# First tile loaded whole with its own weights, second tile in pieces of 16 and 9 tokens, the other tiles' weights sent behind the first store

## The chip, the cores and the metric

The kernel runs on one core of one Trainium2 chip. The metric is the device time of one execution in microseconds (us). A tensor lies in the chip's main memory (HBM) and is worked on in the core's own memory (SBUF), which has 128 partitions. VectorE (DVE in the profile) and ScalarE (ACT) multiply; 16 DMA engines carry data between the two memories. A transfer is issued by the sequencer of an engine: here SyncE (SP) issues the stores and the weights, on the queue that the profile calls q1, and ScalarE issues the loads of `x`, on q10.

## The reference

Each token's row of 512 numbers is copied for each of its two experts and multiplied by that expert's weight. The expert indices are not used.

```python
batch, seq, hidden, n_experts = 16, 1024, 512, 8
k = 2
x_expanded = x[:, :, np.newaxis, :].repeat(k, axis=2)
weights = expert_weights[..., np.newaxis]
return (x_expanded * weights).astype(np.float32)
```

All is float32. There are 16,384 tokens, so 33.55 MB of `x` and 0.13 MB of weights come in, and 67.11 MB of output go out.

## The kernel before

With 128 partitions, each partition gets 128 tokens. They are cut into five tiles of 25 tokens for each partition (`groups`) and a rest of 3 (`LAST`, held in `z_tile`). Token counts below are always those of one partition. A tile of `x` is 128 rows of 25 × 2,048 bytes, and every transfer has one row for each partition, eight to each of the 16 DMA engines.

The buffers:

- `x_tile`: two buffers in turn, so tile i+2 can be loaded only when tile i has been multiplied.
- `o_ring`: one output buffer, as large as one whole tile's output (25 × 4,096 bytes a partition). Each part of a tile writes to its own range of it, so a part can be written only when the store of the range's last content has landed.
- `w_tile`: the weights of all tiles.

`load(i)` (L68) issues the loads of tile i on ACT's queue. For tile 0 it issues two, of 9 and 16 tokens (`FIRST`, L35), and behind the first of them it has SP issue all three weight transfers (L82-83): `weights(0)` (L95) for tile 0, 50 numbers a partition; `weights(1)` (L97) for tiles 1 to 4, four stretches of 50 numbers a partition; `weights(2)` (L104) for the rest, 6 numbers a partition. Then `load(0)` issues the load of `z_tile` (L85). `load(1)` issues tile 1 in one piece.

The main loop (L156) takes the tiles in order. `emit` (L148) cuts tiles 0 and 1 into 13 and 12 tokens and the later ones into 9, 8 and 8. For each part, `fill` (L142) has VectorE do the first v tokens, in steps of up to four tokens (one `tensor_tensor` each, L127), and ScalarE the rest, with one multiplication for each token and expert (L117). `SHARES` (L36) holds v: 9 of 13 and 8 of 12 in tiles 0 and 1; in later tiles VectorE does all. Then SP issues the part's store (L152). Below, the stores are called 0a and 0b (tile 0), 1a and 1b (tile 1), 2a, 2b, 2c and so on, and z for the last. After a tile's parts, `load(i + 2)` is issued from ACT's queue, which therefore stands behind that tile's multiplications on ScalarE.

Each queue is served in the order of issue: on SP the three weight transfers, then the stores in order; on ACT the loads of tile 0, z, tile 1, and then tiles 2, 3 and 4 as their buffers come free.

Of the kernel before, what the change touches and what calls it, by code (L numbers as in the profile page):

```python
# [1 line left out]

# [4 lines left out]


@with_exitstack
def kernel(  # L10
    ctx: ExitStack,
    tc: tile.TileContext,
    x: bass.AP,
    expert_indices: bass.AP,
    expert_weights: bass.AP,
    out: bass.AP,
):
    nc = tc.nc

    batch, seq, hidden = x.shape  # L20
    k = expert_weights.shape[-1]
    P = nc.NUM_PARTITIONS
    ntok = batch * seq
    assert ntok % P == 0
    A_TOTAL = ntok // P

    f32 = mybir.dt.float32
    row = k * hidden
    CH = 4


    groups = [25, 25, 25, 25, 25]
    TX = max(groups)
    LAST = 3
    FIRST = [9, 16]  # L35
    SHARES = [[9, 8], [9, 8], [9, 8, 8]]  # L36
    assert sum(groups) + LAST == A_TOTAL

    xf = x.rearrange("b s h -> (b s) h")
    of = out.rearrange("b s k h -> (b s) (k h)")  # L40
    wf = expert_weights.rearrange("b s k -> (b s) k")

    w_pool = ctx.enter_context(tc.tile_pool(name="w_pool", bufs=1))
    x_pool = ctx.enter_context(tc.tile_pool(name="x_pool", bufs=2))
    o_pool = ctx.enter_context(tc.tile_pool(name="o_pool", bufs=1))

    w_tile = w_pool.tile([P, A_TOTAL * k], f32)
    o_ring = o_pool.tile([P, TX * row], f32)

    def rows(of_all, done, T):  # L50
        return of_all[done * P : (done + T) * P, :].rearrange(
            "(p a) n -> p (a n)", a=T
        )


    if LAST:
        z_pool = ctx.enter_context(tc.tile_pool(name="z_pool", bufs=1))
        z_tile = z_pool.tile([P, LAST * hidden], f32)

    tiles = []  # L60
    done = 0
    for n in groups:
        tiles.append((done, n))
        done += n

    loaded = []

    def load(i):  # L68
        if i >= len(tiles):
            return  # L70
        done, n = tiles[i]
        x_tile = x_pool.tile([P, TX * hidden], f32)
        src = rows(xf, done, n)
        steps = FIRST if i == 0 else [n]
        for e, step in enumerate(steps):
            at = sum(steps[:e])
            nc.scalar.dma_start(
                out=x_tile[:, at * hidden : (at + step) * hidden],
                in_=src[:, at * hidden : (at + step) * hidden],
            )  # L80
            if i == 0 and e == 0:
                for g in range(3):  # L82
                    weights(g)
        if i == 0 and LAST:
            nc.scalar.dma_start(out=z_tile, in_=rows(xf, A_TOTAL - LAST, LAST))  # L85
        loaded.append(x_tile)


    T0 = groups[0]
    G = len([n for n in groups[1:] if n == T0])  # L90
    head = (1 + G) * T0

    def weights(e):
        if e == 0:
            nc.sync.dma_start(out=w_tile[:, : T0 * k], in_=rows(wf, 0, T0))  # L95
        elif e == 1:
            nc.sync.dma_start(  # L97
                out=w_tile[:, T0 * k : head * k].rearrange("p (g n) -> p g n", g=G),
                in_=wf[T0 * P : head * P, :].rearrange(
                    "(g p a) n -> p g (a n)", g=G, p=P  # L100
                ),
            )
        else:
            nc.sync.dma_start(  # L104
                out=w_tile[:, head * k :], in_=rows(wf, head, A_TOTAL - head)
            )

    def product(engine, o_tile, t, x_in, c, m):

        o = t * row  # L110
        if engine is not None:
            for e in range(m * k):
                out_e = o_tile[:, o + e * hidden : o + (e + 1) * hidden]
                in_e = x_in[:, e // k * hidden : (e // k + 1) * hidden]
                w_e = w_tile[:, c + e : c + e + 1]
                if engine is nc.scalar or engine is nc.any and (c + e) % 3 == 2:
                    nc.scalar.mul(out=out_e, in_=in_e, mul=w_e)  # L117
                else:
                    nc.vector.tensor_scalar(
                        out=out_e,  # L120
                        in0=in_e,
                        scalar1=w_e,
                        scalar2=None,
                        op0=mybir.AluOpType.mult,
                    )
            return
        nc.vector.tensor_tensor(  # L127
            out=o_tile[:, o : o + m * row].rearrange(
                "p (t k h) -> p t k h", t=m, k=k
            ),  # L130
            in0=x_in[:, : m * hidden]
            .rearrange("p (t h) -> p t h", t=m)
            .unsqueeze(2)
            .to_broadcast([P, m, k, hidden]),
            in1=w_tile[:, c : c + m * k]
            .rearrange("p (t k) -> p t k", t=m)
            .unsqueeze(3)
            .to_broadcast([P, m, k, hidden]),
            op=mybir.AluOpType.mult,
        )  # L140

    def fill(o_tile, x_in, c, m, v):  # L142
        for t in range(0, v, CH):
            u = min(t + CH, v)
            product(None, o_tile, t, x_in[:, t * hidden : u * hidden], c + t * k, u - t)
        product(nc.scalar, o_tile, v, x_in[:, v * hidden :], c + v * k, m - v)

    def emit(src, dst, c, cuts, shares):  # L148
        for at, to, v in zip(cuts, cuts[1:], shares):
            o_tile = o_ring[:, at * row : to * row]  # L150
            fill(o_tile, src[:, at * hidden : to * hidden], c + at * k, to - at, v)
            nc.sync.dma_start(out=dst[:, at * row : to * row], in_=o_tile)  # L152

    for i in range(2):
        load(i)
    for i, (done, n) in enumerate(tiles):  # L156
        cuts = [0, 13, n] if i < 2 else [0, 9, 17, n]
        emit(loaded[i], rows(of, done, n), done * k, cuts, SHARES[min(i, 2)])
        load(i + 2)
    emit(  # L160
        z_tile,
        rows(of, A_TOTAL - LAST, LAST),
        (A_TOTAL - LAST) * k,
        [0, LAST],
        [LAST],
    )

# [1 line left out]
_INS = ['x', 'expert_indices', 'expert_weights']  # L169
_OUTS = [((16, 1024, 2, 512), 'float32')]  # L170


# [23 lines left out]
```

## Time and profile before

| What | Value |
|---|---|
| Time, median of 3 runs | 240.13 us (239.79 to 240.28) |
| Time of the profiled execution | 240.12 us |
| Span of the profiled execution | 238.3 us |
| VectorE busy | 122.6 us (51% of the span), 32 instructions |
| ScalarE busy | 21.2 us (9%), 33 instructions |
| Queue q1 (stores, weights) | 67.24 MB, 65.5% of 16 DMA engines' span |
| Queue q10 (loads of `x`) | 33.55 MB, 33.2% |

The span is the stretch of time in which the profiled program does something that the profile records; the execution's own time is 1.8 us longer. A DMA "share" is the mean busy share of the 16 DMA engines. A transfer's packets are counted at the time at which they start, so a short window can show more than 1.00. The rows that the argument rests on stand in the prediction.

### The profile page before, as it was taken

The page shows a single profiled execution, that of the slowest core. Times are in us where ns is not written, and L with a number is a line of the kernel's source. Part 1 is how long each engine was busy: PE and PEld are TensorE (multiplying, and loading weights), DVE is VectorE, ACT ScalarE, POOL GpSimd, SP SyncE. Part 2 cuts the span into 40 slices and gives each one's busy share as a digit, 9 for nine tenths or more (in the row PEclk, how much of TensorE's full clock was granted, in tenths as well). Part 3 has the DMA queues.
Part 4 walks back from the last instruction along what each step waited for, and adds up shares of the span by engine and source line. Part 5 has one row for each costly group of instructions (what it writes and reads, how often), then busy time and mean ns, then how long its engine had stood idle before and what let it go on. Part 6 is the DMA issues. An engine that isn't in the chain of part 4 may idle for free.

```text
span 238.3 us, 167 instructions
## 1 busy us (share of the span) xinstructions
DVE 122.6 (51%) x32; ACT 21.2 (9%) x33; POOL 0.2 (0%) x4
## 2 busy tenths in 40 slices
DVE  0599600000069292099405999493086999865000
ACT  0008900000061250000000000000000000000000
POOL 0000000000000000000000000000000000000000
DMA  7999999999999999999999999999999999999996
GB/s 264 465 386 504 457 414 413 413 424 429 429 396 429 472 465 426 422 404 405 412 484 431 402 434 444 414 434 425 449 408 461 434 440 431 421 413 423 440 434 264
DMA packets 3840, 100.80 MB, mean 423 GB/s; under 512 B 1152, under 2 KB 1152, under 8 KB 1280
## 3 DMA queue, kind: packets, MB, share of 16 engines
q1 hardware_dynamic: 2832, 67.24, 65.5%
q10 hardware_dynamic: 1008, 33.55, 33.2%
HBM read 33.69 MB, written 67.11 MB: 423 GB/s over the span
## 4 chain that ended last, share of the span: by engine, by line
DMA 58%; DVE 28%; issue 2%; another core or an unknown queue 2%; ACT 1%; DVEq 0%; SPq 0%
DMA out_dram<-o_ring 55%; DVE o_ring L127 28%; DMA x_tile<-in_x_dram 3%; ACT o_ring L117 1%; DVEq L127 0%; SPq L152 0%
## 5 line engine op out<-in xcount | busy, mean ns | idle before, releaser
L127 DVE TENSOR_TENSOR o_ring<-x_tile,w_tile 128x4096 f32<-128x4096 f32 (+1 forms) x31 | 119.3, 3905 | 93.2 <-DMA out_dram<-o_ring 82.3
L117 ACT ACTIVATE o_ring<-x_tile,w_tile 128x512 f32<-128x512 f32 x32 | 19.9, 708 | 47.1 <-DMA out_dram<-o_ring 47.0
L127 DVE TENSOR_TENSOR o_ring<-z_tile,w_tile 128x3072 f32<-128x3072 f32 x1 | 3.4, 3359 | 2.1 <-DMA out_dram<-o_ring 2.1
L117 ACT ACT_TABLE_LOAD x1 | 1.3, 1283 | 18.7 <-DMA x_tile<-in_x_dram 18.7
L180 POOL MEMSET const-uint8-127<- 128x1 uint8 x1 | 0.1, 102 | 0.0
L180 POOL MEMSET const-bfloat16-1.0<- 128x1 bf16 x1 | 0.1, 101 | 0.0
L180 POOL MEMSET const-float32-0.0<- 128x1 f32 x1 | 0.1, 98 | 0.2 <-issue 0.2
L180 POOL MEMSET const-float32-1.0<- 128x1 f32 x1 | 0.1, 98 | 0.0
## 6 DMA issues: line engine op xcount, KB each, us to landing
x_tile<-in_x_dram ACTq DMA_DIRECT2D x4, 6400.0 KB, 31.6
out_dram<-o_ring SPq DMA_DIRECT2D x6, 4096.0 KB, 21.5
out_dram<-o_ring SPq DMA_DIRECT2D x3, 4608.0 KB, 27.3
out_dram<-o_ring SPq DMA_DIRECT2D x2, 6656.0 KB, 33.1
out_dram<-o_ring SPq DMA_DIRECT2D x2, 6144.0 KB, 44.5
x_tile<-in_x_dram ACTq DMA_DIRECT2D x1, 4096.0 KB, 17.5
x_tile<-in_x_dram ACTq DMA_DIRECT2D x1, 2304.0 KB, 8.1
out_dram<-o_ring SPq DMA_DIRECT2D x1, 1536.0 KB, 19.5
```

What stands on the lines that cost most here:

```text
L117: nc.scalar.mul(out=out_e, in_=in_e, mul=w_e)
L127: nc.vector.tensor_tensor(out=o_tile[:, o : o + m * row].rearrange("p (t k h) -> p t k h", t=m, k=k), in0=x_in[:, : m * hidden] .rearrange ...
L180: nc = _bacc.Bacc("TRN2", target_bir_lowering=False, num_devices=1)
```

## The change

Tile 0 is loaded in one piece, and tile 1 in two, of 16 and 9 tokens. The weights go in four transfers in place of three: tile 0's and tile 1's, 50 numbers a partition each, behind the load of tile 0; those of tiles 2 to 4 (three stretches of 50 numbers) and of the rest (6) are issued by SP right behind store 0a. To hold them there, ScalarE copies 156 numbers a partition out of tile 0 into the place of `w_tile` where they will land, after its part of 0a; both transfers overwrite the copied numbers. The load of `z_tile` moves from behind tile 0 to behind tile 1. VectorE's tokens change from 9 and 8 to 7 and 7 in tile 0, and from 9 and 8 to 10 and 9 in tile 1; ScalarE does the other tokens of the 13 and 12.

On SP's queue the order is now: weights of tile 0, weights of tile 1, store 0a, weights of tiles 2 to 4, weights of the rest, store 0b, and then the stores as before. On ACT's: load of tile 0, both loads of tile 1, z, and the later tiles as before. Beside the buffers' own waits, SP's instruction for the weights of tiles 2 to 4 waits for the copy on ScalarE.

```diff
-    FIRST = [9, 16]
-    SHARES = [[9, 8], [9, 8], [9, 8, 8]]
+    STEPS = {1: [16, 9]}
+    SHARES = [[7, 7], [10, 9], [9, 8, 8]]
...
-        steps = FIRST if i == 0 else [n]
+        steps = STEPS.get(i, [n])
         for e, step in enumerate(steps):
             at = sum(steps[:e])
             nc.scalar.dma_start(
...
             if i == 0 and e == 0:
-                for g in range(3):
-                    weights(g)
-        if i == 0 and LAST:
+                weights(0)
+                weights(1)
+        if i == 1 and LAST:
             nc.scalar.dma_start(out=z_tile, in_=rows(xf, A_TOTAL - LAST, LAST))
...
     def weights(e):
-        if e == 0:
-            nc.sync.dma_start(out=w_tile[:, : T0 * k], in_=rows(wf, 0, T0))
-        elif e == 1:
+        if e < 3:
+            at, to = ((0, T0), (T0, 2 * T0), (2 * T0, head))[e]
+            g = (to - at) // T0
             nc.sync.dma_start(
-                out=w_tile[:, T0 * k : head * k].rearrange("p (g n) -> p g n", g=G),
-                in_=wf[T0 * P : head * P, :].rearrange(
-                    "(g p a) n -> p g (a n)", g=G, p=P
+                out=w_tile[:, at * k : to * k].rearrange("p (g n) -> p g n", g=g),
+                in_=wf[at * P : to * P, :].rearrange(
+                    "(g p a) n -> p g (a n)", g=g, p=P
                 ),
             )
...
             nc.sync.dma_start(out=dst[:, at * row : to * row], in_=o_tile)
+            if c == 0 and at == 0:
+                nc.scalar.copy(
+                    out=w_tile[:, 2 * T0 * k :],
+                    in_=src[:, : (A_TOTAL - 2 * T0) * k],
+                )
+                weights(2)
+                weights(3)
```

## The prediction

> **What bounds the kernel now.** I read the page first: the busy times, then the strip of 40 slices.
>
> ```profile
> DVE 122.6 (51%) x32; ACT 21.2 (9%) x33; POOL 0.2 (0%) x4
> ...
> DMA  7999999999999999999999999999999999999996
> GB/s 264 465 386 504 457 414 413 413 424 429 429 396 429 472 465 426 422 404 405 412 484 431 402 434 444 414 434 425 449 408 461 434 440 431 421 413 423 440 434 264
> ...
> HBM read 33.69 MB, written 67.11 MB: 423 GB/s over the span
> ```
>
> The busiest compute engine is idle half the time; the DMA engines are full in all slices but the first and the last. The strip is coarse, so I asked for windows chosen by stage (the columns that matter are the last two: DMA share and GB/s).
>
> ```profile
> 0.00:1.70 1.70, 0.00 (x0) 0.00 (x0) 0.20 (x4) 1.00 0.00 0
> 1.70:3.50 1.80, 0.00 (x0) 0.00 (x0) 0.00 (x0) 1.00 1.03 328
> ...
> 6.90:25.00 18.10, 16.17 (x5) 6.25 (x10) 0.00 (x0) 1.00 1.02 435
> 25.00:50.60 25.60, 2.45 (x1) 4.94 (x9) 0.00 (x0) 1.00 0.99 417
> 50.60:90.90 40.30, 18.66 (x5) 10.01 (x16) 0.00 (x0) 1.00 1.01 436
> 90.90:150.00 59.10, 36.30 (x10) 0.00 (x0) 0.00 (x0) 1.00 1.00 431
> 150.00:200.00 50.00, 34.01 (x10) 0.00 (x0) 0.00 (x0) 1.00 1.00 432
> 200.00:235.00 35.00, 15.04 (x4) 0.00 (x0) 0.00 (x0) 1.00 0.99 429
> 235.00:238.30 3.30, 0.00 (x0) 0.00 (x0) 0.00 (x0) 1.00 0.39 164
> ```
>
> From 1.7 us, where the first packet starts, to 235 us no stage has the DMA engines idle: 0.99 to 1.03 in every window, and 429 to 436 GB/s from 50 us on, with loads mixed in or not. So the end is set by bytes over rate. All 100.80 MB (33.69 + 67.11) at 432 GB/s take 233.3 us; with the 1.7 us ahead that gives 235.0 us. The last window moves 164 × 3.3 = 541 KB, 1.25 us at full rate, so the actual stream ends near 236.3 us. At most about 1.3 us can be gained by any order of the same transfers. The Trainium skill ("DMA: Bandwidth & Descriptors", section "Where 436 GB/s comes from") gives 435 GB/s as the ceiling of 16 ports; by it the bytes need 231.7 us, and 1.6 us more could be had than by my row, none of it by changing an order.
>
> The chain of waits must be read with that in mind.
>
> ```profile
> 0.73 8.08 DMA x_tile<-in_x_dram
> ...
> 8.83 14.98 DVE o_ring L127 x5
> ...
> 25.07 42.40 DMA out_dram<-o_ring
> ...
> 67.59 9.90 DVE o_ring L127 x3
> 77.49 4.48 another core or an unknown queue
> ...
> 82.06 8.77 DVE o_ring L127 x2
> ...
> 90.88 36.96 DMA out_dram<-o_ring
> ```
>
> It alternates between VectorE and stores and looks like a chain that a faster start would shorten. But store 0a, issued at 25.07, lands 42.40 us later though its 6.82 MB need 15.8 us: it stands in a queue. While VectorE works (67.59 to 77.49) the DMA engines are busy with other rows. The chain sets the end only where a queue runs dry.
>
> **The change, part by part.** The sum starts from the profiled execution's own 240.12 us, which is the median of the runs (240.13) to 0.01.
>
> Bytes and rows: the loads have seven transfers before and after, with the same rows in other sizes. Weights have 8 + 32 + 8 = 48 rows on each DMA engine before, and 8 + 8 + 24 + 8 = 48 after, in four transfers instead of three. Cost: 0, apart from what the places do.
>
> The first store. These are the rows of the timeline and of the groups by shape:
>
> ```profile
> 18.74 1.28 ACT L117 ACT_TABLE_LOAD   x1 [18.74 <-DMA x_tile<-in_x_dram]
> 20.03 9.91 ACT L117 ACTIVATE o_ring<-x_tile,w_tile 128x512 f32<-128x512 f32 x16
> ...
> 29.97 0.37 ACTq L77 DMA_DIRECT2D x_tile<-in_x_dram  x1
> ```
>
> ```profile
> L127 DVE TENSOR_TENSOR o_ring<-x_tile,w_tile 128x4096 f32<-128x4096 f32 x26 | 113.8, 4421 | 93.2 <-DMA out_dram<-o_ring 82.3 <-DMA x_tile<-in_x_dram 8.8 <-issue 2.1
> ...
> L127 DVE TENSOR_TENSOR o_ring<-x_tile,w_tile 128x1024 f32<-128x1024 f32 x5 | 6.1, 1219 | 0.0
> L127 DVE TENSOR_TENSOR o_ring<-z_tile,w_tile 128x3072 f32<-128x3072 f32 x1 | 3.4, 3359 | 2.1 <-DMA out_dram<-o_ring 2.1
> ```
>
> Before, all 25 tokens of tile 0 had landed by 18.74; one load lands then too, so VectorE starts at about 18.7 instead of 8.83. Its 7 tokens take 4.42 + 3.36 = 7.8 us (to 26.5); ScalarE's 12 multiplications take 12 × 9.91/16 = 7.4 us (to 26.1, or 27.4 if the table load of 1.28 comes no earlier). Store 0a is issued at about 27 instead of 25.07. What hides this: the loads of tiles 0 and 1 and of z, 53 tokens or 13.89 MB, keep the engines full until 1.7 + 13.89/0.432 = 33.9 us. Cover: 7 us; beyond it each us costs a us.
>
> Then VectorE needs 7.8 us for 0b, to about 34.4, and ScalarE 10 × 0.62. Store 0b and the load of tile 2 (29.97 before) are issued at about 34.4. Now store 0a is the cover: 20.71 MB are done at 49.6 us. Cost 0.
>
> ScalarE's copy of 128x156 has no row: 0 to 0.71 us, the mean of a 128x512 multiplication; I take 0.3 (it has a third of the elements). Behind it on ScalarE stands its part of 0b, which ends by 33.9 (27.4 + 0.3 + 6.2), still ahead of VectorE's. The two weight transfers wait for it on SP; behind them stands store 0b, not ready for another 6 us. All of it costs 0.
>
> Tile 1: store 0a no longer waits behind 48 weight rows and lands near 50 instead of 67.47. VectorE's 10 tokens take 2 × 4.42 and one 128x2048, unseen, between 1.22 and 3.36; I take 2.29, their mean: 11.1 us. So 1a is issued near 61 instead of 77.49. That gains nothing: until about 82 us the engines have the load of tile 2 and store 0b to move. Store 0b can't land earlier, since the same 33.55 MB have to pass ahead of its end as before. It lands at about 82, where part 1b starts as before (82.06). 1b takes 4.42 + 4.42 + 1.22 = 10.1 instead of 8.77 us, so 1b and the load of tile 3 are issued at 92.1 instead of 90.88. Cover: store 1a, alone from 82, lasts 15.8 us, to 97.8; 5.7 us are left. Cost 0. From here on the order of work is as before.
>
> The weight rows in a new place. The answer about the queues in the first 3 us, and the issues there (size, us to landing):
>
> ```profile
> q1 hardware_dynamic: 84, 0.02, 5.1%
> ...
> w_tile<-in_expert_weights_dram SPq DMA_DIRECT2D x1, 100.0 KB, 36.7
> w_tile<-in_expert_weights_dram SPq DMA_DIRECT2D x1, 25.0 KB, 5.3
> w_tile<-in_expert_weights_dram SPq DMA_DIRECT2D x1, 3.0 KB, 50.3
> ```
>
> 84 small rows took 5.1% of 16 engines × 3 us, 29 ns each. That 100 KB take 36.7 us to land shows how rows mix: the queues take turns, and a weight row waits for a row of `x`. Before, loads lay beside all weight rows until 50.3 us after the last one's issue, so their latency was hidden. After, 24 + 8 rows and 2 completion writes stand between stores 0a and 0b, beside at most z's 8 rows and tile 2's 8 on each engine. So about 18 of them run with no partner: 18 × 29 ns = 0.5 us if they pass one after the other, 0 if they overlap with the store rows around them. I take 0.1, near the hidden end, since the rows before them and behind them are long.
>
> The joint between loads and the first store. One window is slower than its neighbours:
>
> ```profile
> 46.35:48.25 1.90, 0.00 (x0) 0.00 (x0) 0.00 (x0) 1.00 1.00 431
> 48.25:50.62 2.37, 0.00 (x0) 0.00 (x0) 0.00 (x0) 1.00 1.05 346
> 50.62:52.58 1.96, 0.00 (x0) 0.00 (x0) 0.00 (x0) 1.00 1.02 435
> ```
>
> The last round of tile 2's rows took 2.37 us instead of 1.90, just ahead of store 0a's first rows: 0.47 us lost. After, store 0a starts among the loads of tile 1, and 0b behind the weights near the end of tile 2's load, the same situation. Bounds: no such joint (-0.47) to one more (+0.47); I take +0.1, because there are two candidates for the one seen.
>
> The start: the first window ran at 328 GB/s, which loses 1.8 × (1 - 328/432) = 0.43 us. First rows of 51 KB instead of 18 KB, and 16 weight rows instead of 48 queued beside them, could change it by as much either way; I take 0.
>
> Sum: 240.12 + 0.1 + 0.1 = 240.3 us.
>
> **Rivals.** A change of 0.2% (0.48 us) is about what a measurement of this kernel can tell from none.
>
> Slower by the small rows, 241.1: the 18 rows without a partner pay the full 0.5 us, and the second joint 0.47. For it: both are new, and nothing in the new order takes a loss away for sure. Against: a saturated stream so far hid 48 such rows. It decides from the point where q10 is empty while the weights stand ahead of store 0b.
>
> The page of the skill named above has a rule against the change (section "Rules for kernel authors": transfers under 64 KB are mostly overhead; section "Anatomy of one DMA — SWDGE": about 2 us fixed for each). As a mechanism here: the added transfer isn't overlapped. Priced by rows, it is at least the 1.0 us from the first issue (0.73) to the first packet (1.7): 241.1 to 241.4. Against: 14 stores in a row leave no gap in the windows after 50 us. By the page's own 2 us it would be 242.1.
>
> Slower by a dry queue, 242 or more: if tile 0 landed 7 us later than 18.7, or 1b came 5.7 us later, the engines would wait, us for us. Nothing in the rows delays either that much.
>
> Faster by cleaner joints, 239.5: the loss at 48.25 goes, and part of the start's 0.43. For it: the weights no longer run beside tile 2's load ahead of store 0a.
>
> Faster by the earlier store 0a (16 us on the chain): excluded by a DMA share of 1.00 while it waits.
>
> **How the numbers follow.** The forecast, no change that can be told, 0.48; small rows 0.27, unoverlapped transfer 0.04, dry queue 0.04, so slower 0.35; faster 0.17. The forecast's own range is 239.7 to 240.8. The predicted range reaches down to the faster case, 239.4, and up past the small-rows case, 241.3.
>
> **What would show it.** Right: DMA share near 1.00 in all windows to 235 us; VectorE's first instruction near 18.7; store 0a issued near 27 and landing near 50; 0b landing near 82; the stores from 2a on at their old times to 1 us. Wrong: a window of some us with a share under 0.9, above all around 34, 65 to 68 and 98 us; or a time under 239.4, which would mean that rows pass faster in the new order than anywhere in this trace.

## The result and the profile after

| | before | changed |
|---|---|---|
| Median | 240.28 us (239.79 to 240.93, 8 runs) | 242.34 us (240.86 to 243.57, 8 runs) |
| Ratio to before, 95% interval | 1 | 1.0082 (1.0060 to 1.0104) |
| Profiled execution | 240.12 us, span 238.3 us | 240.98 us, span 238.8 us |

The change costs 2 us, and the eight executions spread over 2.7 us instead of 1.1. The profiled execution of the changed kernel lies 1.4 us under its median, and all three profiles that I have of it lie low (240.98, 241.59 and 240.89 us, while of the other 17 executions 16 took 242.2 us or more), so most of the loss has to be looked for in variants. Two executions of the variants below (246.72 us of e14, 244.70 us of e15) lay over 1.5% above the shortest of their kernel; the ratios leave them out, the medians do not.

The changed kernel's DMA share and rate in the windows of before:

```profile
0.00:1.70 1.70, 0.00 (x0) 0.00 (x0) 0.20 (x4) 1.00 0.00 0
...
6.90:25.00 18.10, 6.02 (x2) 7.30 (x11) 0.00 (x0) 1.00 0.94 405
25.00:50.60 25.60, 9.28 (x3) 7.79 (x14) 0.00 (x0) 1.00 0.99 416
50.60:90.90 40.30, 19.41 (x5) 7.56 (x12) 0.00 (x0) 1.00 1.01 436
90.90:150.00 59.10, 37.91 (x12) 0.00 (x0) 0.00 (x0) 1.00 1.01 434
150.00:200.00 50.00, 33.39 (x10) 0.00 (x0) 0.00 (x0) 1.00 1.00 429
200.00:235.00 35.00, 15.48 (x4) 0.00 (x0) 0.00 (x0) 1.00 0.99 428
```

From 25 us on the engines are as full as before. (Packets count at their start; the rows of the first load are longer now, which moves bytes into the windows ahead of 6.9 us.) No window shows the engines without work. The timeline gives the times of the steps; columns are start, duration, engine, line and operation, and in brackets the idle time ahead with what ended it:

```profile
11.41 1.28 ACT L117 ACT_TABLE_LOAD   x1 [11.41 <-DMA w_tile<-in_expert_weights_dram]
18.98 15.30 DVE L127 TENSOR_TENSOR o_ring<-x_tile,w_tile 128x4096 f32<-128x4096 f32 x4 [18.98 <-DMA x_tile<-in_x_dram]
...
26.35 0.30 ACT L154 COPY w_tile<-x_tile 128x156 f32<-128x156 f32 x1
...
26.77 0.35 SPq L152 DMA_DIRECT2D out_dram<-o_ring  x1
...
34.37 0.36 ACTq L77 DMA_DIRECT2D x_tile<-in_x_dram  x1
...
51.33 10.96 DVE L127 TENSOR_TENSOR o_ring<-x_tile,w_tile 128x4096 f32<-128x4096 f32 x3 [17.05 <-DMA out_dram<-o_ring]
...
82.45 9.90 DVE L127 TENSOR_TENSOR o_ring<-x_tile,w_tile 128x4096 f32<-128x4096 f32 x3 [20.16 <-issue]
92.43 48.83 ACTq L77 DMA_DIRECT2D x_tile<-in_x_dram  x2
100.12 14.23 DVE L127 TENSOR_TENSOR o_ring<-x_tile,w_tile 128x4096 f32<-128x4096 f32 x4 [7.78 <-DMA out_dram<-o_ring]
127.77 22.90 DVE L127 TENSOR_TENSOR o_ring<-x_tile,w_tile 128x4096 f32<-128x4096 f32 x6 [13.42 <-DMA out_dram<-o_ring]
```

VectorE starts at 18.98, store 0a is issued at 26.77 and has landed by 51.33, part 1b starts at 82.45, tile 3's load is issued at 92.43. These are the forecast's times within 1.4 us. One row answers differently from before: part 2a, which waits for store 1a, starts at 100.12. Before it was

```profile
82.06 8.76 DVE L127 TENSOR_TENSOR o_ring<-x_tile,w_tile 128x4096 f32<-128x4096 f32 x2 [4.57 <-DMA out_dram<-o_ring]
...
101.55 4.43 DVE L127 TENSOR_TENSOR o_ring<-x_tile,w_tile 128x4096 f32<-128x4096 f32 x1 [10.73 <-DMA out_dram<-o_ring]
```

so 19.5 us after the start of 1b; now it is 17.7. The difference, 1.8 us, is about one row of tile 3's load (51 KB at the 432/16 GB/s of one engine are 1.9 us). Tile 3's load, issued about 1.5 us later, seems to get one row fewer in ahead of store 1a's last one. So the order of the rows on the engines did change behind 82 us, where I had written that it would not.

### The profile page after: what moved, and what is told of

Read it like the earlier page. It is cut to its first block, busy times and chain, and to the rows that moved or that the text cites. A ratio compares the mean times of both kernels' runs of the same rounds, so it can differ in the third digit from the quotient of the medians.

```text
span 238.8 us, 177 instructions
## 1 busy us (share of the span) xinstructions
DVE 121.5 (51%) x32; ACT 22.6 (9%) x36; POOL 0.2 (0%) x4
## 4 chain that ended last, share of the span: by engine, by line
DMA 56%; DVE 21%; issue 14%; DVEq 0%; SPq 0%
DMA out_dram<-o_ring 48%; DVE o_ring L127 21%; DMA x_tile<-in_x_dram 8%; DVEq L127 0%; SPq L152 0%
## 5 line engine op out<-in xcount | busy, mean ns | idle before, releaser
L127 DVE TENSOR_TENSOR o_ring<-x_tile,w_tile 128x4096 f32<-128x4096 f32 (+3 forms) x31 | 118.1, 3869 | 94.8 <-DMA out_dram<-o_ring 55.6
L117 ACT ACTIVATE o_ring<-x_tile,w_tile 128x512 f32<-128x512 f32 x34 | 21.2, 707 | 52.1 <-DMA out_dram<-o_ring 45.8
## 6 DMA issues: line engine op xcount, KB each, us to landing
out_dram<-o_ring SPq DMA_DIRECT2D x6, 4096.0 KB, 21.7
out_dram<-o_ring SPq DMA_DIRECT2D x1, 1536.0 KB, 19.5
```

Of the source, the lines that this page charges most:

```text
L127: nc.vector.tensor_tensor(out=o_tile[:, o : o + m * row].rearrange("p (t k h) -> p t k h", t=m, k=k), in0=x_in[:, : m * hidden] .rearrange ...
```

## The experiments

All ratios are against the kernel before, measured beside it on the same chip, in five rounds. A ratio is not the quotient of the two medians; the two can differ by some 0.15%.

### Which part of the change costs the time

Four kernels. The first takes the load order alone, on top of before:

```diff
-    FIRST = [9, 16]
+    STEPS = {1: [16, 9]}
...
-        if i == 0 and LAST:
+        if i == 1 and LAST:
```

> The change's load order alone (tile 0 whole, tile 1 as 16 and 9, z behind it); weights in three transfers at the start and VectorE's shares of 9 and 8 as before. Theory W (the loss comes from the weight rows that stand between stores 0a and 0b with few rows of x beside them): 240.0 to 240.6, as before. Theory L (the loss comes from the load order: long first rows, and loads still running when store 0a starts): about 242, with a spread of over 1 us among the executions. Theory X (both are needed): as before.

The second takes the late weights alone (the changed kernel with `STEPS = {0: [9, 16]}`, z behind tile 0, and the old shares):

> The change's weights alone: those of tiles 0 and 1 at the start, the others behind store 0a, with the copy; loads and shares as before. Theory W: about 242, spread over 1 us. Theory L: 240.0 to 240.6. Theory X: as before.

The third is the changed kernel with all weights at the start:

```diff
                 weights(0)
                 weights(1)
+                weights(2)
+                weights(3)
...
-            if c == 0 and at == 0:
-                nc.scalar.copy(
...
```

> The changed kernel with all four weight transfers at the start and no copy; loads and shares as changed. Theory W: back to 240.0 to 240.6. Theory L: stays at about 242. Theory X: back to before.

The fourth is the changed kernel itself:

> The changed kernel again, for its spread and for a second profile. All theories: median near 242.3, executions between 240.9 and 243.6. If the profile falls on a slow execution (span over 240 us), theory W expects the lost time between stores 0a and 0b (60 to 70 us), theory L between 17 and 50 us; a loss spread evenly over the span would speak against both.

| Run | Loads | Weights late | Shares | Median us | Ratio (95% interval) |
|---|---|---|---|---|---|
| e1_loads | new | no | old | 240.33 | 1.0005 (0.9989 to 1.0021) |
| e2_weights | old | yes | old | 240.12 | 0.9997 (0.9983 to 1.0011) |
| e3_early | new | no, four transfers | new | 242.37 | 1.0079 (1.0050 to 1.0107) |
| e4_again | new | yes | new | 242.70 | 1.0091 (1.0069 to 1.0112) |

Theories W and L both fall: neither the weights nor the load order costs anything alone that shows, and with the weights back at the start the loss stays whole, which takes theory X with it. Left are the shares, or the fourth weight transfer beside the new loads. Four more kernels separate these; they differ only in the line `SHARES` or in the pieces above:

> The change's load order and shares (7 and 7, 10 and 9), with the weights in three transfers at the start as before. Theory S (VectorE's 9 tokens in 1b make it 1.1 us longer, so store 1b and the load of tile 3 are issued 1.1 us later and meet store 1a's last rows): about 242.3. Theory F (the fourth weight transfer beside the new load order does it): 240.2 to 240.6.

> The change's load order with four weight transfers, all at the start, and the old shares of 9 and 8. Theory S: 240.2 to 240.6. Theory F: about 242.3.

> The kernel before with the changed shares alone. Theory S: about 242.3, since 1b is 1.1 us longer here too. A theory that needs the new load order as well: 240.2. Theory F: 240.2.

> The changed kernel with the old shares of 9 and 8 in tiles 0 and 1. Theory S: back to 240.2 to 240.6. Theory F: stays at about 242.3.

| Run | Loads | Weights | Shares | Median us | Ratio (95% interval) |
|---|---|---|---|---|---|
| e5_loads_shares | new | three, early | new | 241.90 | 1.0069 (1.0045 to 1.0093) |
| e6_loads_four | new | four, early | old | 240.60 | 1.0023 (1.0005 to 1.0041) |
| e7_shares | old | three, early | new | 240.83 | 1.0036 (1.0018 to 1.0054) |
| e8_old_shares | new | late | old | 240.40 | 1.0017 (1.0001 to 1.0032) |

The loss follows the shares: one line, `[[7, 7], [10, 9], ...]` back to `[[9, 8], [9, 8], ...]`, takes the changed kernel from 1.0082 to 1.0017. With the old loads the new shares cost half as much (1.0036), so theory S's 242.3 for that case was too high. The profiles offer a reason: with the old loads the new shares bring forward only store 0a (23.85 us instead of 25.07), while store 0b and the load of tile 2 are issued at 29.98 us as before (29.97). Theory F falls, though e6's interval leaves it 0.05 to 0.4%; e8, with the late weights, is no slower than e6, with the early ones.

### Which share, and by what

Variants of the changed kernel. Three change only the numbers in `SHARES`; the other, e11, takes the old shares and holds tile 3's load back with a copy on ScalarE:

```diff
-    SHARES = [[7, 7], [10, 9], [9, 8, 8]]
+    SHARES = [[9, 8], [9, 8], [9, 8, 8]]
...
+        if i == 1:
+            at = 19 * hidden
+            nc.scalar.copy(out=loaded[1][:, at : at + 900], in_=loaded[1][:, :900])
         load(i + 2)
```

> The changed kernel with VectorE's share of part 1b back at 8 tokens (7 and 7, 10 and 8). Theory S1 (it is 1b's ninth token: store 1b and the load of tile 3 are issued 1.1 us later): 240.2 to 240.7. Theory S0 (it is the 7 and 7 of tile 0 or the 10 of 1a): stays at 241.9 to 242.7.

> The changed kernel with the old shares but 9 tokens in part 1b (9 and 8, 9 and 9). Theory S1: 241.9 to 242.7. Theory S0: 240.2 to 240.7.

> The changed kernel with the old shares, and one copy of 128x900 on ScalarE between VectorE's last product of tile 1 and the load of tile 3, into the buffer that this load overwrites; store 1b isn't held. The load of tile 3 is issued about 1.1 us later, store 1b as early as with the old shares. Theory S1 in the form that the load's issue decides: 241.9 to 242.7. In the form that store 1b's issue decides, or both together: 240.2 to 240.7.

> The changed kernel with VectorE's share of 1b at 6 tokens (10 and 6); ScalarE's 12 products then end last, about 7.4 us after the start of 1b instead of 9.9, so store 1b and the load of tile 3 are issued 2.5 us earlier than in the changed kernel. Theory S1, if earlier is better throughout: 240.0 to 240.4. If there is a good place and a bad one by turns (the time goes with the place of these issues among store 1a's rows of 2 us each): anything from 240.0 to 242.7, and not the same as with 8.

| Run | Shares of tiles 0 and 1 | Median us | Ratio (95% interval) |
|---|---|---|---|
| e9_1b_eight | 7, 7; 10, 8 | 241.42 | 1.0046 (1.0032 to 1.0061) |
| e10_1b_nine | 9, 8; 9, 9 | 241.32 | 1.0052 (1.0032 to 1.0072) |
| e11_load_late | 9, 8; 9, 8, load of tile 3 held | 240.85 | 1.0036 (1.0018 to 1.0053) |
| e12_1b_six | 7, 7; 10, 6 | 241.18 | 1.0055 (1.0035 to 1.0074) |

Neither S1 nor S0 alone: taking back the ninth token leaves half of the loss, and adding it to the old shares brings about half. There are two causes of about equal size. What holding the load alone costs lies between none and all of the ninth token's effect: its interval meets those of e8 and of e10. In the profiled executions the load is issued 9.8 us after the start of 1b (92.39 after 82.62) against 8.9 in e8 (91.76 after 82.91). An earlier 1b (e12) is no better than one of 8 tokens.

The next four ask whether it is the time of the issues or the split of the work. In the first two, VectorE repeats one token of 1b once or twice, with the old shares; store and load then come later and the split stays:

```diff
+            if at == 13 and c == 2 * T0 * k // 2:
+                for _ in range(1):
+                    product(None, o_tile, 7, src[:, 20 * hidden : 21 * hidden], c + 40, 1)
             nc.sync.dma_start(out=dst[:, at * row : to * row], in_=o_tile)
```

> The changed kernel with the old shares, and the last token of VectorE's part of 1b computed twice (one more 128x1024 product, 1.2 us, same values): store 1b and the load of tile 3 are issued 1.2 us later, while ScalarE's work stays that of the old shares. Theory T (the place of these two issues in time decides): 241.0 to 241.7, as with nine tokens. Theory A (the split of the work between the engines decides): 240.2 to 240.6.

> The same with that token computed three times: both issues 2.4 us later than with the old shares, a little more than one row of store 1a (2.0 us). Theory T as a matter of phase (the place within a row): back near 240.4. Theory T as a matter of late or early (the less of store 1a is left, the worse): 241.5 or more. Theory A: 240.2 to 240.6.

> The changed kernel with 7 and 7 in tile 0 and the old 9 and 8 in tile 1. If tile 0's shares (stores 0a and 0b and the load of tile 2 issued 2 to 3 us earlier than with 9 and 8) carry the part of the loss that is left with 1b at 8 tokens: 241.0 to 241.5. If 1a's tenth token carries it: 240.4.

> The changed kernel with the old 9 and 8 in tile 0, and 10 and 8 in tile 1. If 1a's tenth token carries the rest of the loss: 241.0 to 241.5. If tile 0's shares do: 240.4.

| Run | Shares of tiles 0 and 1 | Median us | Ratio (95% interval) |
|---|---|---|---|
| e13_one_twice | 9, 8; 9, 8, a token of 1b twice | 241.75 | 1.0051 (1.0027 to 1.0075) |
| e14_two_twice | 9, 8; 9, 8, a token three times | 241.92 | 1.0065 (1.0039 to 1.0090) |
| e15_tile0 | 7, 7; 9, 8 | 241.68 | 1.0053 (1.0031 to 1.0074) |
| e16_1a_ten | 9, 8; 10, 8 | 240.18 | 1.0010 (0.9993 to 1.0027) |

For 1b it is the time of the issues: the same split with the issues 1.2 us later costs as much as the ninth token, and 2.4 us later no less, so it is not a matter of phase that comes back after one row. Part 1a's tenth token costs nothing that shows. Tile 0's 7 and 7 carry the other half. Beside e16, measured with them on one chip, the intervals of e14 and e15 are clear and that of e13 touches; e13's and e15's overlap e8's (1.0001 to 1.0032) by 0.05% or less. The last two kernels: e15 with tile 0's stores put back to their old times,

```diff
             o_tile = o_ring[:, at * row : to * row]
+            if c == 0 and at == 0:
+                product(None, o_ring, 13, src[:, 5 * hidden : 7 * hidden], 10, 2)
```

> The kernel of e15 (7 and 7 in tile 0, 9 and 8 in tile 1), with one more product of 128x2048 on VectorE ahead of everything (2.3 us; it writes values of tokens 5 and 6 where part 0b's first product writes over them). Stores 0a and 0b and the load of tile 2 are then issued about as late as with the old shares (near 29 and 37 us instead of 27 and 34), while the split between VectorE and ScalarE stays 7 and 7. Theory T (the time of these issues decides): 240.2 to 240.7. Theory A (the split decides): 241.3 to 242.1, as e15.

> The changed kernel once more, for a profile of a slow execution. If the lost time is one DMA engine that falls behind: the median engine ends near 237 us also in an execution of 242 or more, and in the last 2 us of the stream the DMA share is about 1/16 = 0.06. If all engines lose alike: the share stays near 1 to the end, and windows in the middle are below 425 GB/s.

| Run | Median us | Ratio (95% interval) |
|---|---|---|
| e17_tile0_late | 240.81 | 1.0025 (1.0009 to 1.0042) |
| e18_changed | 242.56 | 1.0094 (1.0072 to 1.0115) |

The profiles show when store 0a is issued, in e8, e15 and e17:

```profile
28.78 0.35 SPq L152 DMA_DIRECT2D out_dram<-o_ring  x1
26.82 0.35 SPq L152 DMA_DIRECT2D out_dram<-o_ring  x1
29.10 0.35 SPq L154 DMA_DIRECT2D out_dram<-o_ring  x1
```

e17 lies with e8 and not with e15, as the time of the issue would have it; the intervals of e15 and e17 overlap a little, so for tile 0 this is likely and not as firm as for 1b. e18's profile again fell on the fastest of its executions (240.89 us; the other five took 242.25 to 243.76), so its question is answered by the variants and, in part, by e4's profile.

### Where the lost time lies

The end of the stream, in windows, of the kernel before:

```profile
233.00:235.00 2.00, 0.00 (x0) 0.00 (x0) 0.00 (x0) 1.00 0.99 424
235.00:236.50 1.50, 0.00 (x0) 0.00 (x0) 0.00 (x0) 1.00 0.83 352
236.50:237.10 0.60, 0.00 (x0) 0.00 (x0) 0.00 (x0) 1.00 0.05 20
237.10:237.70 0.60, 0.00 (x0) 0.00 (x0) 0.00 (x0) 1.00 0.00 0
```

of e15_tile0, whose profiled execution took 242.44 us:

```profile
233.00:235.00 2.00, 0.00 (x0) 0.00 (x0) 0.00 (x0) 1.00 0.98 418
235.00:236.50 1.50, 0.00 (x0) 0.00 (x0) 0.00 (x0) 1.00 0.79 336
236.50:237.10 0.60, 0.00 (x0) 0.00 (x0) 0.00 (x0) 1.00 0.15 61
237.10:237.70 0.60, 0.00 (x0) 0.00 (x0) 0.00 (x0) 1.00 0.14 61
237.70:238.50 0.80, 0.00 (x0) 0.00 (x0) 0.00 (x0) 1.00 0.11 46
238.50:240.00 1.50, 0.00 (x0) 0.00 (x0) 0.00 (x0) 1.00 0.02 8
```

of e13_one_twice (241.87 us):

```profile
236.50:237.10 0.60, 0.00 (x0) 0.00 (x0) 0.00 (x0) 1.00 0.39 164
237.10:237.70 0.60, 0.00 (x0) 0.00 (x0) 0.00 (x0) 1.00 0.19 82
237.70:238.50 0.80, 0.00 (x0) 0.00 (x0) 0.00 (x0) 1.00 0.07 31
```

and of the changed kernel itself in its longest profile, e4_again (241.59 us):

```profile
236.50:237.10 0.60, 0.00 (x0) 0.00 (x0) 0.00 (x0) 1.00 0.15 61
237.10:237.70 0.60, 0.00 (x0) 0.00 (x0) 0.00 (x0) 1.00 0.05 20
237.70:238.50 0.80, 0.00 (x0) 0.00 (x0) 0.00 (x0) 1.00 0.04 15
```

One engine of 16 is a share of 0.06. In e15 most engines end where they ended before, near 236.5 us. Then 0.15 to 0.11 is left for 2 us: two engines still have their last rows to move, and then one. The whole stream was as fast as before, and one or two engines are late. In e13 the engines end one after another, the last one alone, and in e4 one engine is alone from 237.1 us on.

Where the lag came up can be read on VectorE, because a store has landed only when its last engine is done. These rows are the starts of 1b (after store 0b), 2a (after 1a) and 2b's second half (after 1b), of e8_old_shares:

```profile
82.91 8.76 DVE L127 TENSOR_TENSOR o_ring<-x_tile,w_tile 128x4096 f32<-128x4096 f32 x2 [20.53 <-issue]
102.47 14.23 DVE L127 TENSOR_TENSOR o_ring<-x_tile,w_tile 128x4096 f32<-128x4096 f32 x4 [10.80 <-DMA out_dram<-o_ring]
128.23 8.76 DVE L127 TENSOR_TENSOR o_ring<-x_tile,w_tile 128x4096 f32<-128x4096 f32 x2 [11.53 <-DMA out_dram<-o_ring]
```

of e13_one_twice:

```profile
82.89 10.02 DVE L127 TENSOR_TENSOR o_ring<-x_tile,w_tile 128x4096 f32<-128x4096 f32 x3 [18.64 <-issue]
100.58 14.23 DVE L127 TENSOR_TENSOR o_ring<-x_tile,w_tile 128x4096 f32<-128x4096 f32 x4 [7.67 <-DMA out_dram<-o_ring]
129.73 8.76 DVE L127 TENSOR_TENSOR o_ring<-x_tile,w_tile 128x4096 f32<-128x4096 f32 x2 [14.92 <-DMA out_dram<-o_ring]
```

and of e15_tile0:

```profile
84.30 8.76 DVE L127 TENSOR_TENSOR o_ring<-x_tile,w_tile 128x4096 f32<-128x4096 f32 x2 [21.82 <-issue]
103.89 14.23 DVE L127 TENSOR_TENSOR o_ring<-x_tile,w_tile 128x4096 f32<-128x4096 f32 x4 [10.83 <-DMA out_dram<-o_ring]
129.87 8.76 DVE L127 TENSOR_TENSOR o_ring<-x_tile,w_tile 128x4096 f32<-128x4096 f32 x2 [11.74 <-DMA out_dram<-o_ring]
```

In e15, where tile 0's issues are early, store 0b lands 1.4 us later than in e8 although the same bytes were ahead of it: the lag was there by 84 us, and 2b is late by about the same (129.87 against 128.23). In e13, where 1b's issues are late, 0b lands as in e8 (82.89) and store 1b 1.5 us later (129.73): the lag came up while tile 3's load ran beside store 1b. Also, 1a lands 17.7 us after 0b in e13, as in the changed kernel, and 19.6 in e8 and e15: the one row of tile 3's load. Each lag arises in the stage that its edit touches, and both are edits that the changed kernel has.

These are single executions, but the packet records of the other traces agree. Each transfer leaves sixteen records of 4 bytes, as many as there are engines (272 on q1 for the 17 transfers of before); I read them as its ends on the sixteen engines. The table has, for three stores, how long the last of them came behind their median, and when the median ended the stream (all in us):

| Run (profiled execution) | Store 0b | Store 1b | Store z | End of the median |
|---|---|---|---|---|
| before (240.12) | 0.32 | 0.63 | 0.76 | 236.44 |
| e8_old_shares (240.66) | 0.89 | 0.86 | 1.17 | 236.52 |
| e15_tile0 (242.44) | 2.63 | 2.68 | 2.79 | 236.37 |
| e13_one_twice (241.87) | 0.95 | 2.36 | 2.15 | 236.75 |
| e11_load_late (241.92) | 0.67 | 2.19 | 2.36 | 236.58 |
| e4_again (241.59) | 1.36 | 1.62 | 1.85 | 236.36 |
| changed (240.98) | 0.56 | 0.50 | 0.59 | 237.02 |
| e3_early (243.05) | 1.32 | 1.96 | 2.25 | 237.53 |

Beside the new loads, five of the eight profiles with 7 and 7 in tile 0 have a lag of 1.32 to 2.63 us at store 0b. None of the eight with 9 and 8 has over 0.95, and e17, with 7 and 7 but late issues, has 0.55. From 0b to 1b the lag grows by 0.79 us or more in e10, e11, e13 and e14, and by at most 0.64 in all others, the changed kernel's own profiles among them. The changed kernel's profile of 240.98 us has both moved issues and the 17.7 us, and no lag: the moved issues make the lag likelier, they do not force it, and the one row that passes is not itself the loss.

The records also show what held the late engine. An engine's next packet starts where its last one ended, so it can be followed back. The last engine of e15 has most of its lag from four rows, which started at 30.2, 49.1, 51.5 and 66.4 us and took 1.0, 0.5, 0.3 and 0.9 us longer than usual for their size; three are rows of loads. That of e13 lost its 1.4 us between 0b and 1b in four rows of tile 3's load, started between 100 and 120 us, that took 0.3, 0.3, 0.3 and 0.6 us longer than the usual 1.89.

One execution lost time in another way as well. In e3_early (243.05 us) the rate dipped where tile 3's load meets the joint of stores 1a and 1b:

```profile
90.00:96.00 6.00, 2.98 (x2) 0.00 (x0) 0.00 (x0) 1.00 0.98 426
96.00:102.00 6.00, 1.30 (x1) 0.00 (x0) 0.00 (x0) 1.00 0.96 318
102.00:108.00 6.00, 6.00 (x2) 0.00 (x0) 0.00 (x0) 1.00 1.08 469
```

The share stays at 0.96 while the rate falls to 318 GB/s: the packets in flight take longer. The next window has 469 because of where its packets start; the two together are at 394 GB/s. Before, the same two windows have

```profile
96.00:102.00 6.00, 0.45 (x1) 0.00 (x0) 0.00 (x0) 1.00 0.97 411
102.00:108.00 6.00, 6.00 (x2) 0.00 (x0) 0.00 (x0) 1.00 0.96 401
```

a mean of 406, so by these windows e3 lost about 0.4 us there in 12. The packet records say more: the rows that started from 84 to 128 us took 21.7 us longer in sum than is usual for their sizes, 1.4 us for each engine, against 4.5 us in sum before. The difference, 1.1 us for each engine, is also what e3's median engine ends later than that of before (237.53 against 236.44).

## Why the prediction was wrong

The times of the steps were right: 18.7 forecast and 18.98 measured for VectorE's start, 27 and 26.77 for store 0a's issue, 34.4 and 34.37 for tile 2's load, near 50 and 51.33 for 0a's landing, 92.1 and 92.43 for tile 3's load. So was the cover: the DMA share shows no queue running dry, and the dry-queue rival fell, though its 242 us or more is what was measured; that is chance. The earlier landing of store 0a (16 us) gained nothing, as said.

Wrong was the price put on the moved issues. The step that failed is "5.7 us are left. Cost 0. From here on the order of work is as before." The cover hides a late issue from the engines as a group. It does not keep their balance: in the profiles of e13 and e15 the last of the 16 engines ends 2.15 and 2.79 us behind the median one, which ends within 0.3 us of where it did before. Store 1b and tile 3's load, about 1.1 us later, cost 0.35%, or 0.8 us (e10 and e13 less e8: 1.0052 and 1.0051 to 1.0017); the issues of tile 0, 2 to 3 us earlier than with the old shares and also put at 0 under "The first store", as much again (e15 less e8). Against before these are later, not earlier, and with the old shares later still (store 0a at 28.78 us in e8) at next to no cost, so it is not a matter of late or early alone. I took the sixteen engines as one, with a mean rate, while a finer window of before (0.05 from 236.5 to 237.1 us) shows one of them alone at the end even there.

The two small terms, +0.1 each, were aimed at the wrong places. The weight rows between stores 0a and 0b cost nothing that shows: e2 is at 0.9997, and e3, without them, is as slow as the changed kernel. The small-rows rival had the sign of the result and 241.1 us, and its mechanism is not what made the loss (e8, with the rows in their new place beside the new loads, leaves it 0.3% at most). The unoverlapped transfer, at 1.0 us, is refuted too by e2, which has all four weight transfers (upper end 1.0011, 0.26 us); e6 leaves room for up to 0.4% beside the new loads. The Trainium skill ("DMA: Bandwidth & Descriptors", section "Anatomy of one DMA — SWDGE") gives its 2 us for transfers that GpSimd issues, while SP issues these; they don't show in this full queue, and that 242.1 us is near the median is chance.

The joint between loads and stores was the right kind of place (e3's window at 96 us is one, and the long rows of e13 and e15 lie where loads run beside stores), but its bounds of ±0.47 us came from one execution. The range ended at 241.3 and the median is at 242.34: a spread between executions was nowhere in the sum. The start, put at 0, no run tests by itself.

What stays open: why some rows take longer, and why more of that falls on one engine when these issues move. The runs show that the loss depends on when loads and stores are issued, how much it costs and in which stage the lag arises; how store 1b and tile 3's load share the effect they do not separate. For tile 0 the evidence of the issue time is e17 alone. And no execution of the changed kernel near its median was profiled: e4's, at 241.59 us, has the lag in part, and e3's shows that all engines together can lose about 1 us as well.

## What to carry to other kernels

When the DMA engines are full from end to end, an edit on VectorE that is hidden behind them need not be free if it moves the time at which transfers are issued: let the range reach up by about one row's time on one engine (here 2 us), for a move either way. The moves here cost between nothing that shows (e16) and 0.8 us each. Look at the last windows of the stream for a share near 1/16, and at landings that come later than the bytes ahead of them ask for; both show one late engine that a mean rate hides. A profiled execution can be the fastest of its kind: compare medians of several, and the spread.

## What the runs showed of the hardware

Of sixteen DMA engines that share the work evenly, the last can end 2.8 us behind the median one (e15: 2.79 us after 236.37), against 0.76 us in the kernel before. The 384 weight rows of 200 bytes for tiles 2 to 4 cost nothing that could be measured in either place (e6 1.0023 with them at the start, e8 1.0017 with them behind store 0a). And 1.2 us more of one VectorE product, hidden behind full engines, moved the whole by 0.3% (e13, 1.0051, against e8, 1.0017).
